# Second FFN of a decoder layer: products of a seven-product scheme ordered by kind, with shared sums in one PSUM bank

## The chip, the cores and the metric

The kernel runs on one core of one Trainium2 chip. The metric is device microseconds of one execution. Three runs of the kernel before took 2109.22, 2109.67 and 2110.75 us.

## The reference

One layer of a decoder over T = 272 positions (16 meta tokens and 256 tokens), width 2048, float32:

```
u = rms_norm(h, ffn1_norm_g);  h = h + 0.5 * swiglu(u, gate1, up1, down1)      # D_FF = 5632
u = rms_norm(h, mix_norm_g);   z = u @ w_in                                    # q k v, indexer, conv, gates
h = h + (sigmoid(ga) * y_attn + sigmoid(gc) * y_conv) @ w_out
u = rms_norm(h, ffn2_norm_g);  h = h + 0.5 * swiglu(u, gate2, up2, down2)
swiglu(x) = (silu(x @ w_gate) * (x @ w_up)) @ w_down
```

Only the last 256 positions are returned. The change is in the last line, the second FFN, which works on those 256 positions alone: two halves of 128 tokens.

## The kernel before, in words

**Products.** Every float32 operand is split into a high and a low part (`hi` a copy rounded to the matmul's type, `lo` what is left), and one product is three matmuls: hi·hi, hi·lo, lo·hi (`trio`, L407 to L410). In the second FFN the stationary operand is a 128x128 block of activations and the moving one 512 columns of weights.

**Quads.** The work is cut into quads: two 128-row blocks of the contraction, two token halves, two 512-column halves of the weights. A plain quad takes 8 products, 24 matmuls. A mixed quad uses the Winograd form of Strassen's scheme: 7 products P1 to P7, 21 matmuls, on sums of activations (`combos`, made in the kernel) and sums of weights (made by `job` during the earlier stages and kept in a scratch buffer in HBM, tiles `made` and `sums`).

**Stages.** The FFN's 5632 inner columns are taken in two groups (`GROUPS = 6, 5`). Each group has 6 or 5 up parts of 8 quads (gate columns and up columns together, 512 each), whose result is gated, transposed and kept in `mid`, and then two down parts (d = 0 and d = 2) of 12 or 10 quads that contract over `mid`. An up part's result f is used by quads 2f and 2f + 1 of the down parts. Before the change the first up part mixes quad 5, every other up part quads 1, 3, 5, 6, the down parts 4 and 4 (first group) and 3 and 5 (second): 57 mixed quads.

**The stream.** Weights come by SP's queue, 1 MB at a time at most, into four raw buffers (three `raw`, one `raws`; `load_one`, L152). A step of the stream (`subs`, `Stream.next`, L211) is up to two blocks of 128x512. `split` (L167 to L176) makes `whi` on ACT and then `wlo` on DVE, for the step three ahead of the one that PE is about to do; there are four pairs of split buffers. A plain step is 4 products (12 matmuls), a mixed step 2 products (6 matmuls), both of them 1024 columns to split. In the kernel before a mixed quad has four steps A to D, of which B is one block.

**Order on an engine.** Each engine runs its instructions in the order in which the program issues them. `st.put(fn, slot)` queues work by slots counted from the step at which it is called: slot 2k is issued at the begin of step k, before the split that step k issues (that of step k + 3), slot 2k + 1 behind that split. `LAG` holds the slots.

**Around the products.** `spread` (L764) adds the products P1, P5, P6, P7 of a part out of four PSUM banks of their own into the four quarters of `u`; `gather` (L776) adds those to the four result banks `c`: DVE, 1024 columns and twice 512. `silu` (ACT, twice 512), `times` (DVE, 1024 columns) and `turn_gated` with `move_blocks` (DVE transposes and DMAs by POOL) follow. The last up part of a group is transposed by DVE alone: `turn_columns` (L626; four transposes L513 in each of four calls, at `last_turn`), then `split_last` (L463 to L465, at `last_split`). `down_combos` makes the activation sums of the down parts: five DVE operations (L702 to L706) and, at a later slot, the split of the results (L689).

Of the kernel before, what the change touches and what calls it, by code (L numbers as in the profile page):

```python
# [67 lines left out]
MIXED = 1, 3, 5, 6  # L68
FIRST_MIXED = 5,
FIFTH = 4  # L70
FIVE = ()
LAST_MORE = 3, 4
JOBS_FROM = 24
JOBS_EVERY = 5
JOBS = 46
LATE_FROM = 4
LATE_EVERY = 6
DOWN_MIXED = {6: (6, 8, 9, 10), 5: (5, 6, 7)}
RAW = 2048
LAG = dict(  # L80
    spread=(0, 0, 1, 1), gather=(0, 0, 0), silu=(1, 1), times=(1,), turn=(1, 1), move=4, hi=(28, 33),
    lo=(28, 33), last_times=(1,), last_turn=(5, 5, 8, 10), last_split=12, half=(3, 3), drain=(2, 4, 3),
    act_combos=(4, 12, 19, 32), factors=(7, 10, 12), out=(1, 1, 5, 17), act_split=(9, 14, 25, 33),
    below=(12, 17, 22, 30, 34), below_split=(15, 20, 30, 34, 35), fifth=(22, 25), late_below=(0, 5),
    late_split=(0, 6),
# [3 lines left out]
def order(n, mixed):  # L89

    out, i = [], 0
    while i < n:
        if i not in mixed:
            out += [(i, "0"), (i, "1")]
        else:
            out += [(i, x) for x in "ABCD"]
        i += 1
    return out


def down_mixed(g, d):
    return sorted((*DOWN_MIXED[GROUPS[g]], *(LAST_MORE if g and d else ())))


class Stream:
# [28 lines left out]
    def add_part(self, name, src, made=None):  # L134

        def load(x):
            self.loads.append((x, x.shape[1], ()))
            return len(self.loads) - 1

        if name in "0A":  # L140
            self.own = load(src if name == "0" else src[:, HALF:]), name == "A" and load(made)
        g = self.own[name in "CD"]
        a, b = {"0": (0, 2), "1": (2, 4), "A": (0, 2), "B": (2, 3), "C": (0, 2), "D": (2, 4)}[name]
        self.subs.append((lambda: self.raw[g][:, a * HALF : b * HALF], b - a, HALF, (g,) if name in "1BD" else ()))
# [91 lines left out]
def tile_decoder_layer(  # L236
# [18 lines left out]
    wgu2: bass.AP,  # L255
    wd2: bass.AP,
# [30 lines left out]
    gu = down = 0  # L287
    made = []
    scratch = ctx.enter_context(tc.tile_pool(name="scratch", bufs=1, space=bass.MemoryType.DRAM))
    for g, n in enumerate(GROUPS):  # L290
        for f in range(n):
            now = sorted((*MIXED, *(FIFTH,) * ((g, f) in FIVE))) if gu else FIRST_MIXED
            sums = {i: scratch.tile([P, RAW], F32, name=f"made{gu + i}") for i in now}
            made += [(wgu2[gu + i], x) for i, x in sums.items()]
            for i, name in order(8, now):
                st.add_part(name, wgu2[gu + i], sums.get(i))
            gu += 8
        for d in (0, 2):
            now = down_mixed(g, d)
            sums = {i: scratch.tile([P, RAW], F32, name=f"sums{down + i}") for i in now}  # L300
            made += [(wd2[down + i], x) for i, x in sums.items()]
            for i, name in order(2 * n, now):
                st.add_part(name, wd2[down + i], sums.get(i))
            down += 2 * n
# [14 lines left out]
    rope = const.tile([P, 3, ROPE], F32, name="rope")  # L319
    cbias = const.tile([P, BOTH], F32, name="cbias")  # L320
    ident = const.tile([P, P], F32, name="ident")
    ones = const.tile([P, P], F32, name="ones")
    const.tile([P, 88], F32, name="fill")
# [19 lines left out]
    def tables():  # L343
# [5 lines left out]
    st.later(tables, 16)  # L349
# [57 lines left out]
    def trio(ps, x, w, first, last):  # L407
        nc.tensor.matmul(ps, x(0), w[0], start=first, stop=False)  # L408
        nc.tensor.matmul(ps, x(0), w[1], start=False, stop=False)  # L409
        nc.tensor.matmul(ps, x(1), w[0], start=False, stop=last)  # L410

    def quads(c, m, x, mixed, n, after_mixed, tail=False):

        def of(k, j):
            return lambda part: x(k, j, part)

        plan, joined = [], []
        for i, name in order(n, mixed):
            k = 2 * i
            if name in "01":  # L420
                unit = [(c[j, q], of(k + int(name), j), 1 - q) for j in (1, 2) for q in (1, 0)]
                if tail and i == n - 1:
                    unit = [] if name == "0" else [
                        (c[j, q], of(k + u, j), 2 * u + 1 - q) for j in (1, 2) for q in range(2) for u in range(2)
                    ]
            else:
                s1, s2, s3, s4 = (lambda part, q=q, i=i: mixed[i](q, part) for q in range(4))
                p1, p2, p3, p4 = (m[1], of(k, 1)), (c[1, 0], of(k + 1, 1)), (c[1, 1], s4), (c[2, 0], of(k + 1, 2))
                p5, p6, p7 = (m[5], s1), (m[6], s2), (m[7], s3)
                unit = dict(A=(p1, p3), B=(p2,), C=(p5, p6), D=(p7, p4))  # L430
                unit = [(*p, b) for b, p in enumerate(unit[name])]
            plan.append((unit, i == max(mixed) and name == "D"))
        flat = [id(p[0]) for unit, _ in plan for p in unit]
        at = 0
        blocks = []
        for unit, last in plan:
            blocks = blocks + [st.next()] + st.rest()
            for ps, xx, b in unit:
                trio(ps, xx, blocks[b], id(ps) not in flat[:at], id(ps) not in flat[at + 1 :])
                at += 1  # L440
            blocks = [] if unit else blocks
            if last:
                after_mixed()
# [110 lines left out]
    def job(pool, bufs, src, to, at, every, touch):  # L554
        box = {}

        def load():
            box["x"] = pool[0].tile([P, RAW], F32, name="made", bufs=bufs)
            if touch:
                nc.vector.tensor_copy(box["x"][:, :1], ones[:, :1])  # L560
            nc.gpsimd.dma_start(box["x"], src)

        def sums(n):
            b12, b11, b22, b21 = (box["x"][:, i * HALF : (i + 1) * HALF] for i in range(4))
# [8 lines left out]
        st.later(lambda: nc.gpsimd.dma_start(to, box["x"]), 1, at + every + 4)  # L573

    def ffn_features():
# [3 lines left out]
        with tc.tile_pool(name="ffn1", bufs=2, reuse_waits="tile") as fp:  # L579
# [16 lines left out]
            for i, (src, to) in enumerate(made[:JOBS]):  # L596
                job([fp], 3, src, to, st.at + JOBS_FROM + i * JOBS_EVERY - 1, JOBS_EVERY, i < 3)
# [56 lines left out]
    def ffn_tokens():  # L654

        with ExitStack() as pools:
# [4 lines left out]
            order_of = [*FIRST_MIXED, *(i for i in MIXED if i not in FIRST_MIXED)]  # L661
            comb = fp.tile([P, 3, 3, 2, P], F32R, name="comb")
            kept = {i: [comb[:, n, q] for q in range(3)] for n, i in enumerate(order_of[:3])}
            written = set()

            def known(key, x):
# [3 lines left out]
            mixed = {  # L670
                i: lambda q, part, i=i: known(i, kept[i][q - 1][:, part] if q else halves[:, 2 * i, part, 1])
                for i in MIXED
            }
# [18 lines left out]
            def put(fns, slots):  # L692
                for fn, slot in zip(fns, slots, strict=True):
                    st.put(fn, slot)
# [920 lines left out]
```

## Time and profile before

| | |
|---|---|
| median of three runs | 2109.67 us |
| span of the profiled execution | 2106.9 us |
| PE busy in it | 2098.8 us |
| DVE, ACT, POOL busy | 1582.4, 1058.9, 106.0 us |
| granted TensorE clock | 1.000 in the mean |
| HBM read, written | 504.90, 68.68 MB |

One execution was profiled, with a span of 2106.9 us from its first to its last instruction; the median run is 2.8 us longer, which is what lies around the span and the spread of the runs. Matmul durations overlap in this profile (one of 512 columns is shown as 0.39 us and the next one starts earlier), so the distance of their starts is what a matmul costs.

### The profile page before, as it was taken

How to read it: one execution, taken by the hardware profiler on the slowest of the kernel's cores; microseconds unless marked ns; L12 is line 12 of the kernel's file. 1: busy time of each engine (PE TensorE's matmuls, PEld its weight loads, DVE VectorE, ACT ScalarE, POOL GpSimd, SP SyncE). 2: the span in 40 equal slices, each digit the busy share in tenths (PEclk: the TensorE clock that was granted, in tenths of full speed). 3: DMA queues.
4: the chain of work that ended last, by engine and by line, in shares of the span. 5: the costliest groups of instructions: out<-in, count | busy, mean ns of one | idle time of the engine just before them, and what ended most of it. 6: DMA issues, size and time to landing. Idle time of an engine off the chain costs nothing.

```text
span 2106.9 us, 31863 instructions
## 1 busy us (share of the span) xinstructions
PE 2098.8 (100%) x12731; PEld 1889.9 (90%) x12731; DVE 1582.4 (75%) x2144; ACT 1058.9 (50%) x1342; POOL 106.0 (5%) x207
## 2 busy tenths in 40 slices
PE   9999999999999999999999999999999999999998
PEld 9999999999999999889988888888888888888887
DVE  7676766676776766578679678769788896878897
ACT  6444433344444445565444444456575565566654
POOL 0000000000000000000000000011000000000000
PEclk9999999999999999999999999999999999999999
DMA  7788888888888865445468886667988777799865
GB/s 265 260 320 327 324 315 322 311 337 310 322 313 325 328 224 177 164 159 181 152 216 329 323 301 223 219 233 255 314 314 300 281 268 247 282 306 319 306 250 207
DMA packets 85908, 575.64 MB, mean 273 GB/s; under 512 B 10112, under 2 KB 10880, under 8 KB 23808
## 3 DMA queue, kind: packets, MB, share of 16 engines
q1 hardware_dynamic: 64080, 438.34, 58.4%
q0 software_dynamic: 21104, 134.23, 17.1%
q8 instruction: 99, 1.62, 0.3%
q10 hardware_dynamic: 576, 1.05, 0.1%
q14 instruction: 49, 0.40, 0.1%
HBM read 504.90 MB, written 68.68 MB: 272 GB/s over the span
## 4 chain that ended last, share of the span: by engine, by line
PE 98%; DVE 1%; DMA 1%; issue 0%; ACT 0%; DVEq 0%; ACTq 0%
PE three L409 5%; PE three L408 5%; PE three L410 5%; PE pd L375 4%; PE pd L376 4%; PE pd L374 4%; PE pu L374 4%; PE pg L375 4%; PE pg L374 4%; PE pu L375 4%; PE pg L376 4%; PE pu L376 4%; PE pgt L402 3%; PE pgt L404 3%; PE pgt L403 3%; PE one L408 3%
## 5 line engine op out<-in xcount | busy, mean ns | idle before, releaser
L176 DVE TENSOR_TENSOR wlo<-raw,whi 128x1024 fp32r<-128x1024 f32 (+1 forms) x771 | 906.2, 1188 | 464.5 <-ACT whi L175 457.7
L175 ACT ACTIVATE whi<-raw 128x1024 fp32r<-128x1024 f32 (+1 forms) x771 | 786.4, 1030 | 883.4 <-PE pd L375 146.2
L375 PE MATMUL pd<-mid,whi 128*128 128x272 f32 x704 | 201.9, 287 | 0.0
L376 PE MATMUL pd<-mid,wlo 128*128 128x272 f32 x704 | 201.9, 287 | 0.0
L374 PE MATMUL pd<-mid,whi 128*128 128x272 f32 x704 | 201.9, 287 | 0.0
L374 PE MATMUL pu<-act,whi 128*128 128x272 f32 x672 | 192.8, 287 | 0.0
L376 PE MATMUL pu<-act,wlo 128*128 128x272 f32 x672 | 192.7, 287 | 0.0
L376 PE MATMUL pg<-act,wlo 128*128 128x272 f32 x672 | 192.7, 287 | 0.0
L375 PE MATMUL pg<-act,whi 128*128 128x272 f32 x672 | 192.7, 287 | 0.0
L375 PE MATMUL pu<-act,whi 128*128 128x272 f32 x672 | 192.7, 287 | 0.0
L374 PE MATMUL pg<-act,whi 128*128 128x272 f32 x672 | 192.7, 287 | 0.0
L568 DVE TENSOR_TENSOR made<-made 128x512 f32<-128x512 f32 x228 | 156.3, 685 | 0.0
L408 PE MATMUL three<-whi,act 128*128 128x512 f32 x352 | 137.2, 390 | 0.1
L409 PE MATMUL three<-wlo,act 128*128 128x512 f32 x352 | 137.0, 389 | 0.0
L410 PE MATMUL three<-whi,act 128*128 128x512 f32 x352 | 137.0, 389 | 0.0
L376 PEld LDWEIGHTS pd<-mid,wlo 128*128 128x128 f32 x704 | 132.7, 188 | 0.0
L374 PEld LDWEIGHTS pd<-mid,whi 128*128 128x128 f32 x704 | 132.7, 188 | 0.0
L375 PEld LDWEIGHTS pd<-mid,whi 128*128 128x128 f32 x704 | 132.7, 188 | 0.0
L176 DVE TENSOR_TENSOR wlo<-raws,whi 128x1024 fp32r<-128x1024 f32 x92 | 103.5, 1140 | 31.7 <-ACT whi L175 31.0
L374 PEld LDWEIGHTS pu<-act,whi 128*128 128x128 f32 x672 | 126.7, 188 | 0.0
L374 PEld LDWEIGHTS pg<-act,whi 128*128 128x128 f32 x672 | 126.7, 188 | 0.0
L376 PEld LDWEIGHTS pg<-act,wlo 128*128 128x128 f32 x672 | 126.6, 188 | 0.0
(381 smaller groups left out, 4482.7 us busy)
## 6 DMA issues: line engine op xcount, KB each, us to landing
raw<-in_wgu_dram SPq DMA_DIRECT2D x123, 1024.0 KB, 6.4
raw<-in_wd_dram SPq DMA_DIRECT2D x63, 1024.0 KB, 6.7
made<-in_wgu_dram POOLq DMA_DIRECT2D x41, 1024.0 KB, 10.6
made<-made POOLq DMA_DIRECT2D x41, 1024.0 KB, 6.5
raw<-made SPq DMA_DIRECT2D x31, 1024.0 KB, 6.1
raw<-in_wcv_dram SPq DMA_DIRECT2D x24, 1024.0 KB, 4.9
raw<-in_wgc_dram SPq DMA_DIRECT2D x24, 1024.0 KB, 5.1
raw<-in_wga_dram SPq DMA_DIRECT2D x24, 1024.0 KB, 5.4
```

The costliest lines, as they stand in the source:

```text
L175: nc.scalar.activation(hi[:, :n], raw, AF.Copy)
L176: nc.vector.tensor_sub(lo[:, :n], raw, hi[:, :n].bitcast(F32))
L374: nc.tensor.matmul(ps, whi, xhi, start=first, stop=False)
L375: nc.tensor.matmul(ps, whi, xlo, start=False, stop=False)
L376: nc.tensor.matmul(ps, wlo, xhi, start=False, stop=last)
L402: nc.tensor.matmul(ps, xhi, whi, start=k + i == 0, stop=False)
L403: nc.tensor.matmul(ps, xhi, wlo, start=False, stop=False)
L404: nc.tensor.matmul(ps, xlo, whi, start=False, stop=k + i == n - 1)
L408: nc.tensor.matmul(ps, x(0), w[0], start=first, stop=False)
L409: nc.tensor.matmul(ps, x(0), w[1], start=False, stop=False)
L410: nc.tensor.matmul(ps, x(1), w[0], start=False, stop=last)
L568: getattr(nc.vector, f"tensor_{op}")(to, a, b)
```

## The change

- `MIXED` is quads 0 to 3 of every up part but the first, which is plain; the down parts mix quads 0 to 3 each (`DOWN_MIXED`). That is 56 mixed quads.
- Within a part the mixed products come by kind: P1 of the four quads, P2 of the four, P6, P7, P5, P4, P3, two blocks in every step, and no step of one block. In an up part (`mixed_first`) they stand ahead of the plain quads, with P4 and P3 among the first of these; in a down part (`plain_first`) behind `lead` plain steps: 14 and 8 steps in the first group, 10 and 4 in the second.
- P1, P6, P5 (and P7 in the down parts) accumulate in one bank `m`; between kinds ACT copies it to a quarter of `u` (`copies`). In an up part `m` is the result bank `c[2, 1]`, and P7 starts in `c[2, 0]`. `spread`'s three DVE operations go; a down part gets two of 512 columns.
- Slots: `times` at 3, `turn_gated` and `move_blocks` in the plain steps of the next part, `last_turn` 9, 9, 11, 13 in place of 5, 5, 8, 10, `last_split` 14 in place of 12; the down sums of quad i at step 7 + 2i, their split at step 8 + 2i.
- Weights of the second FFN lie in HBM in the order of the stream (`w2`); the sums of a part lie in one scratch tile, by kind.

```
-MIXED = 1, 3, 5, 6
-FIRST_MIXED = 5,
-DOWN_MIXED = {6: (6, 8, 9, 10), 5: (5, 6, 7)}
+MIXED = 0, 1, 2, 3
+DOWN_MIXED = (4, 4), (4, 4)
-    spread=(0, 0, 1, 1), gather=(0, 0, 0), silu=(1, 1), times=(1,), turn=(1, 1), move=4, hi=(28, 33),
-    lo=(28, 33), last_times=(1,), last_turn=(5, 5, 8, 10), last_split=12, half=(3, 3), drain=(2, 4, 3),
-    below=(12, 17, 22, 30, 34), below_split=(15, 20, 30, 34, 35), fifth=(22, 25), late_below=(0, 5),
+    silu=(1, 1), times=(3,), last_turn=(9, 9, 11, 13), last_split=14, drain=(0, 2, 4), below=7,
...
+def mixed_first(mixed, plain):
+    own = in_twos(of_kind("P1", mixed) + of_kind("P2", mixed))
+    made = in_twos(sum((of_kind(x, mixed) for x in ("P6", "P7", "P5", "P4")), []))
+    rest = in_twos(of_kind("P3", mixed) + sum(plain_pairs(plain), []))
+    early = -(-3 * len(mixed) // 2)
+    seq = [("h", x) for x in own] + [("m", x) for x in made[:early]]
+    made = made[early:]
+    for i, x in enumerate(rest):
+        seq.append(("h", x))
+        if i >= 2 and i % 2 == 0 and made:
+            seq.append(("m", made.pop(0)))
+    return seq
+def plain_first(mixed, plain, lead):
+    pairs = plain_pairs(plain)
+    seq = [("h", x) for x in pairs[:lead]]
+    pairs = pairs[lead:]
+    seq += [("h", x) for x in in_twos(of_kind("P1", mixed) + of_kind("P2", mixed))]
+    for name in ("P6", "P7", "P5", "P4"):
+        seq += [("m", x) for x in in_twos(of_kind(name, mixed))]
+        if name in ("P6", "P7"):
+            seq.append(("h", pairs.pop(0)))
+    seq += [("h", x) for x in in_twos(of_kind("P3", mixed))]
+    return seq + [("h", x) for x in pairs]
...
+            out.append((("down", g, d), mixed, plain_first(mixed, plain, left - 2 if not d else left - 8)))
...
+            def copy(to, bank):
+                return lambda: st.put(lambda: nc.scalar.activation(u[:, to], bank, AF.Copy), 0)
...
+                        copies = dict(P1=copy(1, m), P6=copy(2, m), P7=copy(3, c[2, 0]), P5=copy(0, m))
...
+                for i in range(max(DOWN_MIXED[g])):
+                    at = LAG["below"] + 2 * i
+                    put_combos(middle, i, home(i), (g, i), 2 * at, 2 * at + 2)
...
+                    copies = dict(P1=copy(0, m), P6=copy(2, m), P7=copy(1, m), P5=after)
...
+        st.later(
+            lambda: nc.gpsimd.dma_start(to, box["x"].rearrange("p (t c) -> p t c", t=4)), 1, at + every + 4
+        )
```

## Rows read from the trace of the kernel before

**Rows 1.** The page, part 1: busy us (share of the span), instructions.
```profile
PE 2098.8 (100%) x12731; PEld 1889.9 (90%) x12731; DVE 1582.4 (75%) x2144; ACT 1058.9 (50%) x1342; POOL 106.0 (5%) x207
```
**Rows 2.** The page, part 4: the chain that ended last, by engine.
```profile
PE 98%; DVE 1%; DMA 1%; issue 0%; ACT 0%; DVEq 0%; ACTq 0%
```
**Rows 3.** Waits of PE: who for whom, us in total, times, longest.
```profile
PE three L409 <- DVE wlo L176: 1.1, 2, 0.8
PE three L408 <- ACT whi L175: 0.3, 1, 0.3
```
**Rows 4.** Timeline of PE, first and last of the second FFN: start, us, instruction.
```profile
1418.94 0.39 PE L408 MATMUL one<-whi,act 128*128 128x512 f32 x1
...
2101.14 0.39 PE L410 MATMUL two<-whi,mid 128*128 128x512 f32 x1
```
**Rows 5.** Chain in order of time: the same matmul of successive up parts.
```profile
1495.27 0.24 PE one L408
...
1576.94 0.24 PE one L408
```
**Rows 6.** Chain in order of time near 2072 us: a late load.
```profile
2072.36 8.25 DMA raw<-sums
```
**Rows 7.** Timeline of PE where one up part ends and the next begins.
```profile
1502.39 0.39 PE L410 MATMUL three<-whi,act 128*128 128x512 f32 x1
1502.62 0.39 PE L408 MATMUL one<-whi,act 128*128 128x512 f32 x1
```
**Rows 8.** Timeline of ACT there (idle before, and what ended it).
```profile
1502.82 0.64 ACT L175 ACTIVATE whi<-raw 128x512 fp32r<-128x512 f32 x1 [1.66 <-PE three L410]
1504.43 1.34 ACT L788 ACTIVATE few<-few,rcol 128x512 f32<-128x512 f32 x2 [0.98 <-DVE few L780]
1505.67 1.05 ACT L175 ACTIVATE whi<-raw 128x1024 fp32r<-128x1024 f32 x1
```
**Rows 9.** Timeline of DVE there: gather, and splits back to back.
```profile
1503.17 1.22 DVE L780 TENSOR_TENSOR few<-three,u 128x1024 f32<-128x1024 f32 x1
1504.31 0.68 DVE L781 TENSOR_TENSOR u<-one,u 128x512 f32<-128x512 f32 x1
1504.91 0.68 DVE L782 TENSOR_TENSOR u<-two,u 128x512 f32<-128x512 f32 x1
1505.50 0.68 DVE L176 TENSOR_TENSOR wlo<-raw,whi 128x512 fp32r<-128x512 f32 x1
...
1508.59 4.59 DVE L176 TENSOR_TENSOR wlo<-raw,whi 128x1024 fp32r<-128x1024 f32 x4
```
**Rows 10.** Timeline of ACT in the second group's first down part.
```profile
2001.40 1.06 ACT L175 ACTIVATE whi<-raw 128x1024 fp32r<-128x1024 f32 x1 [1.41 <-PE three L410]
...
2013.40 1.06 ACT L464 ACTIVATE mid<-mt 128x1024 fp32r<-128x1024 f32 x1 [2.83 <-DVE mt L513]
```
**Rows 11.** Timeline of DVE there: transposes, last split, sums of quad 5.
```profile
2002.50 1.22 DVE L176 TENSOR_TENSOR wlo<-raw,whi 128x1024 fp32r<-128x1024 f32 x1 [0.23 <-ACT whi L175]
2003.64 3.57 DVE L513 STREAM_TRANSPOSE mt<-few 32x256 f32<-32x256 f32 x8
...
2014.54 1.22 DVE L465 TENSOR_TENSOR mid<-mt,mid 128x1024 fp32r<-128x1024 f32 x1
2015.67 0.69 DVE L702 TENSOR_TENSOR few<-mid 128x512 f32<-128x512 f32 x1
...
2017.33 1.22 DVE L176 TENSOR_TENSOR wlo<-raws,whi 128x1024 fp32r<-128x1024 f32 x1
...
2019.60 0.29 DVE L689 TENSOR_TENSOR mid<-few,mid 128x128 fp32r<-128x128 f32 x1
...
2020.27 0.69 DVE L176 TENSOR_TENSOR wlo<-raw,whi 128x512 fp32r<-128x512 f32 x1
```
**Rows 12.** Busy time by stretch: us, engines, PEclk, DMA share, GB/s.
```profile
1484.30:1489.80 5.50, 5.50 (x26) 4.57 (x25) 2.84 (x4) 3.26 (x4) 0.00 (x0) 1.00 1.01 425
2064.00:2080.00 16.00, 16.00 (x72) 13.26 (x71) 12.52 (x12) 10.06 (x11) 0.00 (x0) 1.00 0.82 260
```
**Rows 13.** Waits of POOL: its stores of weight sums.
```profile
POOL made L573 <- DVE made L568: 541.5, 41, 14.3
```

More of the change, by code (lines that the diff above doesn't have):

```diff
@@ L89, in order @@
[L89 to L97, printed above, removed]
-    return out
-def down_mixed(g, d):
-    return sorted((*DOWN_MIXED[GROUPS[g]], *(LAST_MORE if g and d else ())))
+    silu=(1, 1), times=(3,), last_turn=(9, 9, 11, 13), last_split=14, drain=(0, 2, 4), below=7,
+    act_combos=(6, 10, 14, 18, 23), act_split=(9, 13, 17, 21, 25), factors=(7, 10, 12), out=(1, 1, 5, 17),
+)
@@ L105, with loads_of @@
+def loads_of(seq):
+    loads, open_of = [], {}
+    for at, (kind, blocks) in enumerate(seq):
+        x = open_of.get(kind)
+        full = x and sum(len(seq[i][1]) for i in x[1]) + len(blocks) > RAW // HALF
+        if x is None or full or at - x[1][-1] > 4:
+            x = open_of[kind] = (kind, [])
+            loads.append(x)
+        x[1].append(at)
+    return loads
 class Stream:
@@ L132, in add, with add_plan @@
             self.subs.append((view, b - a, width, (g,) if b == n else ()))
[L134 to L144, printed above, removed]
+    def add_plan(self, seq, host, made):
+        at = 0
+        where = {}
+        for kind, subs in loads_of(seq):
+            n = sum(len(seq[i][1]) for i in subs) * HALF
+            if kind == "h":
+                src = host(n)
+            else:
+                src, at = made[:, at : at + n], at + n
+            g = len(self.loads)
+            self.loads.append((src, n, ()))
+            a = 0
+            for i in subs:
+                where[i] = g, a, (g,) if i == subs[-1] else ()
+                a += len(seq[i][1])
+        for i, (_, blocks) in enumerate(seq):
+            g, a, done = where[i]
+            n = len(blocks)
+            self.subs.append((lambda g=g, a=a, n=n: self.raw[g][:, a * HALF : (a + n) * HALF], n, HALF, done))
     def load_one(self, between=(), queues=()):
@@ L405, in tokens, with trio @@
             k += len(blocks)
[L407 to L412, printed above, removed]
+    def trio(ps, x, w, first, last, halting):
+        for i, (a, b) in enumerate(((0, 0), (0, 1), (1, 0))):
+            nc.tensor.matmul(
+                ps, x(a), w[b], start=first and i == 0, stop=last and i == 2, skip_group_check=halting
+            )
@@ L414, in of, with quads @@
+    def quads(c, m, x, s, mixed, seq, copies, last=False):
         def of(k, j):
             return lambda part: x(k, j, part)
[L417 to L425, printed above, removed]
-            else:
[L427 to L432, printed above, removed]
@@ L738, in down_combos @@
[L738 to L746 removed]
+                )
+                his, los, _ = home()
@@ new lines, in combos, with of_combos, of, view @@
+                return sums, split
+            def of_combos(x, home, key):
+                def of(i, q):
+                    def view(part):
+                        if not q:
+                            return known(key(i), x[:, 2 * i, part, 1])
+                        return known(key(i), home(i)()[2](q, part))
+                    return view
+                return of
+            def put_combos(x, i, home, key, slot, late):
+                sums, split = combos(x, i, home, key)
+                for fn in sums:
+                    st.put(fn, slot)
+                st.put(split, late)
```

413 lines of the change are left out of this document (234 added, 179 removed).

## The prediction

> **What bounds the kernel now.** I read the page's busy times first: PE is busy for all but 8 of 2106.9 us, DVE for three quarters [rows 1]. The chain of waits says the same: 98% of what ends last is PE [rows 2]. Then the waits of PE: in the whole second FFN it stood idle for 1.4 us [rows 3]. So a change here can gain little, unless it takes matmuls away, and can lose as much as it makes PE wait. Next comes the price of a matmul, from starts. The same matmul of two up parts lies 1576.94 - 1495.27 = 81.67 us apart over two parts [rows 5]. A part with 4 mixed and 4 plain quads has 4 x 21 + 4 x 24 = 180 matmuls, so one costs 81.67 / 360 = 0.227 us. A mixed step (6 matmuls) is 1.36 us, a plain one (12) 2.72 us. The 57 mixed quads of 132 make 132 x 24 - 57 x 3 = 2997 matmuls. Their starts span 2101.14 - 1418.94 = 682.2 us [rows 4]; 2996 x 0.2269 = 679.7, so 2.5 us are waits. The largest lies behind one late load [rows 6].
>
> **What the change does to PE's own work.** One mixed quad fewer is 3 matmuls more: 3 x 0.227 = +0.7 us. Nothing else changes PE's work. Taking away all 2.5 us of old waits gives -2.5: the places where they stood are laid out anew, and what waits there next is counted below. The other end is that they all stay (0).
>
> **Where steps can be late.** PE needs a step's `wlo` at the step's second matmul. The chain behind that: a split buffer comes free when PE ends a step, and ACT starts on it 1502.82 - 1502.62 = 0.20 us after the next step's first matmul [rows 7, 8]. `whi` takes 1.06 [rows 10], and DVE takes 4.59 / 4 = 1.15 us a piece back to back [rows 9]. With four buffers there are three steps of time. Mixed steps leave DVE only 1.36 - 1.15 = 0.2 us each, plain ones 1.57. So what DVE has to do besides counts where mixed steps stand, and the change puts them together: up to twelve in a row at the start of an up part (four P1 and P2, six of P6, P7, P5, two P3), six in a row in a down part.
>
> **Term 1, from mixed up part to up part (8 times: 4 in each group).** Zero is the first matmul of the new part. DVE may start `gather` at 0.20: 1.14, then twice 0.60 (starts 1503.17, 1504.31, 1504.91, 1505.50 [rows 9]): 2.54. The split of step 3, 1.14: 3.68. ACT meanwhile: `whi` of step 3; `silu` when the first sum is there, 0.20 + 1.22 + 0.04 = 1.46; the two take 1505.67 - 1504.43 = 1.24 [rows 8]: 2.70; `whi` of step 4 until 3.76. DVE: `wlo` 4 from 3.79 to 4.93; then `times`, which the change issues behind it (slot 3): 1.14, 6.07; `wlo` 5 is done at 6.07 + 1.22 = 7.29, handed on at 7.35. PE wants it at 5 x 1.36 + 0.23 = 7.04: **0.3 us late, 8 times: 2.4 us**. In the kernel before two plain steps lay here. Step 6 is in time (DVE gains 0.2 a step). The bounds: 0, if DVE keeps 0.05 us less on each of these six, and 0.6, if it loses as much. The copies of `m` (ACT, as `silu` 0.6) are covered: between a kind's end and the next write of the bank stand two mixed or one plain step, 2.7 us. The three DVE additions that go stood in plain steps, so they give nothing back.
>
> **Term 2, first down part of the second group, the last up part's result.** Its quad 8 is plain and needs up part 4, the last one. It stands at steps 8 and 9 of the ten plain steps ahead. The transposes are issued behind the split of step 7 (slot 9: step 4) and later. Zero is the part's first matmul. Step 3 ends at 4 x 2.72 = 10.90; `whi` of step 7 starts at 11.10. From there on I lay the old trace over it: `whi` 2001.40, `wlo` 2002.50, transposes 2003.64, `split_last` on ACT 2013.40 to 2014.46, on DVE 2014.54 to 2015.76 [rows 10, 11]. The same two splits stand between the sixteen transposes after the change (slots 9, 9, 11, 13). So the transposes start at 11.10 + 2.24 = 13.34, the high half is there at 13.34 + (2014.46 - 2003.64) = 24.16, the low half at 25.46. PE comes to step 8 at 21.8. It waits until 24.2, runs two matmuls, and waits at the third for the low half from 24.66 to 25.5: 2.4 + 0.85 = **3.3 us**. Before, the transposes stood two steps earlier and nothing wanted their result so soon. Bounds 2.4 (the first wait alone) and 3.7.
>
> **Term 3, the same part, the activation sums.** Behind `split_last` DVE has, from 25.4 on, four times the five sums (2017.33 - 2015.67 = 1.66), four times their split (2020.27 - 2019.60 = 0.67) [rows 11], and the `wlo` of steps 10 to 16 between them (7 x 1.14): 6.64 + 2.68 + 7.98 = 17.3, so the sums of quad 3 are split at 42.7. PE ends step 8 at 24.2 + 0.85 + 2.72 = 27.8, step 9 at 30.5, the five mixed steps 10 to 14 at 37.3, and wants quad 3's sum for P6 in the middle of step 15, at 38.0. **4.8 us** of waits between steps 10 and 15. Bounds: 3.5, were the operations 7% shorter; 6.5, as DVE may also have to wait for ACT in that string (the copy of P1 stands behind a split that waits for DVE).
>
> **Term 4, first down part of the first group.** The same string, but with 14 plain steps ahead, and the last up part is first wanted at step 12 (32.7): no wait as in term 2. `wlo` 10 is there at 25.4 + 1.66 + 1.22 = 28.3, wanted at 27.5: 0.8. `wlo` 16 is there at 42.1, wanted, with that shift, at 41.9: 0.2; `wlo` 17, behind quad 3's split in four pieces, at 44.1, wanted at 43.5: 0.6. **1.6 us**, bounds 0.5 and 2.5.
>
> **At nothing.** The first part has DVE's sums in sixteen plain steps. The stores of the weight sums fall into four pieces a row; POOL waits 541.5 us for DVE ahead of those stores [rows 13], and they are wanted hundreds of us later. If that cover were gone, a job would be late, not PE. The end of the kernel is ordered as before.
>
> **Sum.** +0.7 - 2.5 + 2.4 + 3.3 + 4.8 + 1.6 = +10.3 us. Against the profiled execution's 2106.9 that is 2117.2; runs take 2109.67 - 2106.9 = 2.8 more: **2120 us**, +0.5%.
>
> **Loads, and a page against the row.** A mixed step eats 128 x 1024 x 4 bytes in 1.36 us, 385 GB/s, twelve times in a row (6.3 MB), with up to four raw buffers of 1 MB loaded ahead. The trace has 425 GB/s over 5.5 us, but also 260 over 16 us [rows 12], the stretch with the late load. The Trainium skill ("DMA: Bandwidth & Descriptors", Specifications) gives a core some 358 GB/s of HBM; by it the twelve steps would take 17.6 us for 16.3, 1.2 us late in each of 9 up parts, some 11 us, if nothing lay ahead. The 425 speak against that limit here, with one core at work.
>
> **Rivals.**
> - *The string starts earlier* (not slower). If DVE gets to the sixteen transposes two plain steps sooner than I place them (5.4 us), as in the kernel before with slots 5, 5, 8, 10, term 2 and 4 vanish and term 3 too (4.8 < 5.4): +0.7 - 2.5 + 2.4 = +0.6, 2110.3 us. From some 2.5 us on the result is within 0.2% (2.4 + 0.8 + 2.3 - 1.8 = +3.7). For it: the old layout had next to no wait [rows 3]. Against: the diff's slots 9, 9, 11, 13 and the order of DVE.
> - *Loads become the bound.* A wait of 1.4 us, as much as PE idles now in all [rows 3], in each of the 13 mixed parts is +18: with the walked terms 2138, with half of them 2133. For it: 385 wanted, 260 seen. Against: that stretch had five mixed quads with loads of 0.75 and 1 MB; now all are of 1 MB, and plain steps need half as much.
> - *Half of the walk*: terms 1 and 4 are covered, 2 and 3 stay: 2109.7 - 1.8 + 8.1 = 2116.
> - *The mix doesn't bind at all*: no new wait, 2109.7 - 1.8 = 2107.9. That is the floor, and it is within 0.2%: to be faster by that, matmuls would have to start closer than 0.227 us.
>
> **Chances.** About 0.2% (4.2 us) is what a measurement of this kernel tells from no change. As walked 0.60, half of it 0.10, loads 0.10: slower 0.80. Earlier string 0.12, nothing binds 0.04: same 0.16. For a gain that I don't see, faster 0.04. The bounds of the terms give +0.7 - 2.5 + 0 + 2.4 + 3.5 + 0.5 = +4.6 (2114.3) to +0.7 + 4.8 + 3.7 + 6.5 + 2.5 = +18.2 (2127.9). The range for 8 in 10 reaches a little to both other cases: 2112 to 2130.
>
> **What would show it.** Starts of 0.227 us and 3000 matmuls; in each mixed up part but the first a wait of PE for `wlo` at step 5 of some 0.3 us; in the second group's first down part, 22 us behind its begin, a wait for the result of `split_last`, and 8 to 14 us later one for `wlo` or the sums, together 8 us. Wrong, if PE's waits there are under 3 us, if PE waits for raw loads, or if the gain or loss lies ahead of 1419 us.

## The result, and the profile after

The changed kernel takes 2125.12 us (median of 4 runs, 2124.39 to 2126.23), the kernel before 2110.21 on the same chip (4 runs): the ratio is 1.0075, with a 95% interval of 1.0061 to 1.0089. Slower, as forecast, at 2125 where 2120 was said. The traced execution is the one of 2126.23 us.

The page of the changed kernel, its busy times, answers [rows 1], and its chain [rows 2]:

```profile
PE 2108.2 (99%) x12734; PEld 1891.4 (89%) x12734; DVE 1544.3 (73%) x2062; ACT 1072.1 (50%) x1349; POOL 116.1 (5%) x205
```

Its chain that ended last, by engine:

```profile
PE 93%; DVE 4%; issue 2%; ACT 1%; DMA 0%; DVEq 0%; ACTq 0%
```

DVE has 38 us less to do than before and yet a larger part of the chain, 4% for 1%. It isn't how much it has to do, but when. PE's waits in the changed kernel (us in total, times, longest), which answer [rows 3]:

```profile
PE single L470 <- ACT mid L541: 2.3, 1, 2.3
PE single L470 <- DVE wlo L238: 2.1, 5, 0.7
PE single L470 <- ACT act L794: 1.5, 1, 1.5
...
PE single L470 <- DVE mid L542: 0.5, 1, 0.5
PE single L470 <- DVE act L796: 0.5, 1, 0.5
PE double L470 <- DVE wlo L238: 0.3, 1, 0.3
```

L470 is the matmul of the second FFN, L238 the low half of a weight split, L541 and L542 the two halves of `split_last`, L794 and L796 those of the activation sums. No row is a wait for a load. These rows make 7.2 us, and the loss is 15. The rest is seen only in the distance of the starts. First and last matmul of the second FFN (timeline of PE in the changed kernel), which answer [rows 4]:

```profile
1419.47 0.39 PE L470 MATMUL single<-whi,act 128*128 128x512 f32 x1
...
2118.33 0.39 PE L470 MATMUL single<-whi,mid 128*128 128x512 f32 x1
```

3000 starts span 698.9 us for 682.2 before. At 0.2269 us each, what single starts lie further apart than that (where it is more than 0.02 us) sums to 17.9 us, for 2.6 before; taken from the whole span, 698.9 - 2999 x 0.2269, it is 18.4. By place, from the timeline of PE:

| place | us |
|---|---|
| eight transitions from mixed to mixed up part, 0.41 each | 3.3 |
| first mixed up part, steps 4 and 5 | 1.5 |
| first group, first down part | 1.7 |
| second group, first down part: waits for `split_last` | 3.3 |
| the same part: waits in P6 | 3.2 |
| the same part: two stretches in which TensorE ran at half its clock | 4.5 |
| second group, second down part | 0.5 |

**The second group's first down part.** PE in the changed kernel's timeline, the first matmul of the part and then the wait:

```profile
2003.60 0.39 PE L470 MATMUL single<-whi,mid 128*128 128x512 f32 x1
...
2025.13 0.39 PE L470 MATMUL double<-whi,mid 128*128 128x512 f32 x1
2027.78 0.50 PE L470 MATMUL single<-whi,mid 128*128 128x512 f32 x1 [2.26 <-ACT mid L541]
2028.12 0.40 PE L470 MATMUL single<-wlo,mid 128*128 128x512 f32 x1
2029.04 0.79 PE L470 MATMUL single<-whi,mid 128*128 128x512 f32 x1 [0.52 <-DVE mid L542]
2029.63 0.63 PE L470 MATMUL double<-whi,mid 128*128 128x512 f32 x1
2030.06 0.63 PE L470 MATMUL double<-wlo,mid 128*128 128x512 f32 x1
```

DVE there, its transposes, a split between them and the low half of `split_last`, which answer [rows 11]:

```profile
2016.91 3.57 DVE L590 STREAM_TRANSPOSE mt<-few 32x256 f32<-32x256 f32 x8
2020.51 1.22 DVE L238 TENSOR_TENSOR wlo<-raw,whi 128x1024 fp32r<-128x1024 f32 x1
...
2027.76 1.22 DVE L542 TENSOR_TENSOR mid<-mt,mid 128x1024 fp32r<-128x1024 f32 x1 [1.12 <-ACT mid L541]
```

The transposes begin 13.31 us into the part (2016.91 - 2003.60; walked 13.34), PE goes on 24.18 us in (walked 24.2) and gets the low half 25.44 us in (walked 25.46). From the row at 2029.04 on starts lie 0.43 us apart: 2029.63, 2030.06. That is no wait. The windows of the changed kernel say what it is (busy us by engine, PEclk, DMA share, GB/s):

```profile
2024.00:2028.00 4.00, 1.74 (x8) 1.16 (x7) 2.81 (x6) 1.33 (x2) 0.00 (x0) 1.00 0.53 166
2028.00:2032.00 4.00, 3.48 (x9) 2.46 (x9) 3.93 (x9) 2.31 (x4) 0.00 (x0) 0.55 0.23 96
2044.00:2048.00 4.00, 1.73 (x6) 0.60 (x4) 3.93 (x10) 2.31 (x5) 0.00 (x0) 1.00 0.61 199
2048.00:2052.00 4.00, 3.94 (x11) 3.17 (x12) 3.41 (x4) 2.13 (x3) 0.00 (x0) 0.61 0.15 64
```

Behind each stretch in which PE stood for more than half of the time (busy 1.74 and 1.73 of 4 us), the granted clock is down to 0.55 and 0.61 of full in the mean over the next 4 us: in part of them it is at half, 1.2 of 2.4 GHz. Some 14 matmuls behind the first wait and 8 behind the second cost 0.2 us more each, 2.9 + 1.6 = 4.5 us. Before, the clock was 1.00 throughout the second FFN.

**A transition.** The third up part of the first group begins at 1505.41. DVE there, in the timeline of the changed kernel, which answers [rows 9]:

```profile
1505.61 1.23 DVE L875 TENSOR_TENSOR few<-double,u 128x1024 f32<-128x1024 f32 x1 [0.40 <-PE double L470]
...
1510.34 1.22 DVE L892 TENSOR_TENSOR few<-u,few 128x1024 f32<-128x1024 f32 x1
1511.47 1.22 DVE L238 TENSOR_TENSOR wlo<-raws,whi 128x1024 fp32r<-128x1024 f32 x1
```

PE six microseconds on, at step 5 of the part:

```profile
1511.98 0.61 PE L470 MATMUL single<-whi,comb 128*128 128x512 f32 x2
1512.74 0.50 PE L470 MATMUL single<-wlo,comb 128*128 128x512 f32 x1
1513.09 0.40 PE L470 MATMUL single<-whi,comb 128*128 128x512 f32 x1
```

`times` (L892) starts 4.93 us into the part, as walked to the hundredth, and the split of step 5 follows it. PE has two starts by 1512.21 and wants the next at 1512.44; it comes at 1512.74, 0.30 us late. But the one behind it comes only 0.35 us later, not 0.227. That second loss, 0.11 to 0.12 us, stands behind every wait here. The view of waits lists none of the eight: PE is shown busy for 0.61 us from 1511.98, so only 0.15 us of idle time is left in it.

**The first mixed up part**, ACT in the changed kernel's timeline:

```profile
1463.19 1.06 ACT L237 ACTIVATE whi<-raws 128x1024 fp32r<-128x1024 f32 x1 [1.66 <-PE double L470]
1464.27 1.28 ACT L884 ACT_TABLE_LOAD   x1
1465.57 1.27 ACT L884 ACTIVATE few<-double,rcol 128x512 f32<-128x512 f32 x2
```

The first Silu needs a table load of 1.28 us. In the timeline of ACT in the kernel before it stands at the same place, ahead of plain steps, and cost nothing:

```profile
1462.69 1.28 ACT L788 ACT_TABLE_LOAD   x1
```

Now mixed steps follow, and PE waits 0.53 and 0.95 us for their `wlo`. The Trainium skill ("ScalarE: Activation LUTs", What ACT_TABLE_LOAD costs) puts a switch at some 2.66 us, 1.28 for the load and 1.38 for a drain. The row agrees on the load and shows no drain: the split ahead of it ends, and the Silu behind it begins, within 0.02 us of it.

### The profile page after: what moved, and what is told of

Read it like the earlier page. It is cut to its first block, busy times and chain, and to the rows that moved or that the text cites. A ratio compares the mean times of both kernels' runs of the same rounds, so it can differ in the third digit from the quotient of the medians.

```text
span 2124.5 us, 31659 instructions
## 1 busy us (share of the span) xinstructions
PE 2108.2 (99%) x12734; PEld 1891.4 (89%) x12734; DVE 1544.3 (73%) x2062; ACT 1072.1 (50%) x1349; POOL 116.1 (5%) x205
## 4 chain that ended last, share of the span: by engine, by line
PE 93%; DVE 4%; issue 2%; ACT 1%; DMA 0%; DVEq 0%; ACTq 0%
PE single L470 14%; PE double L470 12%; PE pd L437 4%; PE pd L435 4%; PE pd L436 4%; PE pg L436 4%; PE pu L436 4%; PE pu L437 4%; PE pg L437 4%; PE pg L435 4%; PE pu L435 4%; PE pgt L463 3%; PE pgt L465 3%; PE pgt L464 3%; DVE wlo L238 2%
## 5 line engine op out<-in xcount | busy, mean ns | idle before, releaser
L238 DVE TENSOR_TENSOR wlo<-raw,whi 128x1024 fp32r<-128x1024 f32 (+1 forms) x747 | 903.9, 1218 | 507.8 <-ACT whi L237 503.2
L470 PE MATMUL single<-whi,act 128*128 128x512 f32 x592 | 218.0, 389 | 2.0 <-ACT act L794 1.5
L470 PE MATMUL double<-whi,act 128*128 128x512 f32 x544 | 200.3, 389 | 0.0
L470 PEld LDWEIGHTS single<-whi,act 128*128 128x128 f32 x592 | 111.1, 188 | 26.1 <-ACT act L794 1.9
L238 DVE TENSOR_TENSOR wlo<-raws,whi 128x1024 fp32r<-128x1024 f32 x86 | 104.5, 1221 | 32.1 <-ACT whi L237 31.1
L436 PEld LDWEIGHTS pu<-act,whi 128*128 128x128 f32 x672 | 126.6, 188 | 0.0
L435 PEld LDWEIGHTS pu<-act,whi 128*128 128x128 f32 x672 | 126.6, 188 | 0.0
```

What stands on the lines that cost most here:

```text
L238: nc.vector.tensor_sub(lo[:, :n], raw, hi[:, :n].bitcast(F32))
L435: nc.tensor.matmul(ps, whi, xhi, start=first, stop=False)
L436: nc.tensor.matmul(ps, whi, xlo, start=False, stop=False)
L470: nc.tensor.matmul(ps, x(a), w[b], start=first and i == 0, stop=last and i == 2, skip_group_check=halting)
```

## The experiments

The theory: the loss is PE's waits for work of DVE and ACT that now stands too late, each of which another order can cover, and the lower clock is a consequence of the longest of them. The rival: DVE's string of work as a whole sets the pace, and to mend one wait only moves it. Another: the half clock belongs to the mixed steps themselves. On the chip of the first four experiments the kernel before took 2108.2 us, so the changed one, which wasn't run there, would take an estimated 2108.2 x 1.0075 = 2124.0. The waits and the excess are those of one traced execution each. "Excess" is the sum that was 17.9 us above.

**`times` later in mixed up parts.**
```
-  put(times(None if mixed else c), LAG["times"])
+  put(times(None if mixed else c), (11,) if mixed else LAG["times"])
```


> The changed kernel (2125.1 us) with one slot moved: the multiplication `times` of a mixed up part at slot 11 (behind the split issued at step 5) in place of 3. Theory: at the begin of a mixed up part DVE is what is late (gather 2.3 us and times 1.1 us beside splits of 1.14 in steps of 1.36); with times four steps later the 0.41 us waits of PE at step 5 go in all eight parts: -3.3 us, 2121.8, and the trace shows PE waits under 0.1 us there. Rival, the loads are late there: the waits stay, 2125.

2120.77 us, ratio 1.0059 (1.0044 to 1.0074); excess 13.2. All eight waits are gone, 3.3 us. So term 1 is what it was taken for: `times` ahead of the split of step 5. The first of the two stretches at half clock, 2.9 us, is gone too, though the edit doesn't touch it and the wait of 3.3 us in front of it is still there. Of these 2.9 us, 1.4 come back further on in PE's timeline, because PE now reaches P6 earlier:

```profile
2037.03 0.50 PE L470 MATMUL single<-whi,act 128*128 128x512 f32 x1 [1.15 <-ACT u L866]
```

L866 is ACT's copy of the shared bank, and in ACT's order it stands behind the split of an activation sum that waits for DVE.

**The table of Silu loaded early**, by a Silu of two numbers where the norm's factors are made.
```
+  nc.scalar.activation(sums[:, 3], rcol[:, 0, :2], AF.Silu)
```


> The changed kernel with one tiny Silu on two columns added on ACT in the plain steps of the first up part, so that the table load of 1.28 us does not stand before the first real Silu. Theory: the 1.48 us that PE waits at the begin of the first mixed up part (the one stall there that was not foreseen) come from that table load on ACT, which delays whi: they fall to some 0.1 us, -1.4 us, 2123.7. Rival, they come from putting the mixed steps together and DVE's share: they stay, 2125.

2122.25 us, ratio 1.0066 (1.0049 to 1.0083); excess 15.3. The 1.48 us are 0.10 (0.17 more stand in the first part); the transitions stay at 0.42; here too there is one stretch at half clock, not two. The table load was the cause. Two of the four executions of this kernel have a mean clock of 1.000 and no room for such a stretch (the traced one has 0.999): whether the clock falls differs from one execution to the next, so some 1.5 us of any one excess can be chance.

**The last transposes and split one step earlier.**
```
-  last_turn=(9, 9, 11, 13), last_split=14
+  last_turn=(7, 7, 9, 11), last_split=12
```


> The changed kernel with the last up part's transposes and split one plain step (2.72 us) earlier: last_turn 7, 7, 9, 11 and last_split 12. Theory: in the second group's first down part the result of split_last is then there at 21.5 us for the high half (wanted 21.8) and 22.8 for the low (wanted 22.3): the wait of 3.4 us falls to some 0.5, and the TensorE clock, which fell to its lower level behind it for 6.8 us and cost some 2.9 us, does not fall there; behind it the waits for the sums grow, since PE comes earlier, from 3.1 to about 5 us, still with a fall of the clock (1.5 us). In the first group's first down part 1.7 us of waits become under 0.5. Sum -5 us, 2120. Rival, the string of DVE as a whole sets the time and an earlier begin only moves the wait: the two places together (11.0 us now) stay within 1.5 us of that, 2124. Rival, the fall of the clock has nothing to do with the wait: it falls at the same place all the same.

2121.70 us, ratio 1.0063 (1.0048 to 1.0078); excess 13.5. The first group's 1.66 are 0.18, and the second group's wait for `split_last` is 0.67 for 3.33. But behind it 0.57 and 0.43 are new, and P6 has 1.54 and 4.75 (with one stretch at half clock) where the two kernels above have 1.45 and 4.75: of the 2.7 us that an earlier begin gave back at `split_last`, 1.1 are lost again. The two places together make 8.0 us, for 11.0 in the changed kernel and 9.5 in the two runs above, which have one stretch at half clock as well. By the rival they stay within 1.5 us of 11.0: that is refuted by 8.0, but half of the 3.0 us is the stretch at half clock that those two runs lack as well. In time it is 2.3 us under 2124.0, for 4 expected; the four executions lie between 2119.60 (clock 1.000) and 2122.82 (0.998).

**The second group's sums of quads 2 and 3 left out** (their products take those of quads 0 and 1, so part of the result is not the reference's).
```
+  if g and i > 1:
+      continue
...
```


> The changed kernel with half of the activation sums of the second group's down parts left out (quads 2 and 3 use the sums of quads 0 and 1, so part of the computation is wrong). Theory: the waits at P6 (3.1 us, and 1.5 us of the lower clock behind them) come from DVE's sums of quads 2 and 3: they go, -4.5 us, 2120.6; the wait for split_last ahead of it and the lower clock behind that (6.2 us) stay. Rival, they come from the splits of the six mixed steps in a row: most of the 4.7 us stays, 2124.

2119.79 us, ratio 1.0056 (1.0041 to 1.0071); excess 11.9. No wait is left in P6; `split_last` keeps its 3.3 us, now with a stretch at half clock of 1.6 us behind it. Term 3 is DVE's sums: with two of the four left out, ACT's copy of the shared bank comes in time as well.

**All covers at once.** The first three edits in one (`last_turn` 7, 9, 11, 13, `last_split` 15; the second group's sums a step later), and another order for the second group's first down part, in which P4 and P3, which don't use the shared bank, stand between the kinds that do:
```
+  seq = [("h", x) for x in pairs[:8]]
+  seq += [("h", x) for x in in_twos(of_kind("P1", mixed) + of_kind("P2", mixed))]
+  seq += [("h", x) for x in pairs[8:]]
+  for name in ("P6", "P4", "P7", "P3", "P5"):
+      seq += [("h" if name == "P3" else "m", x) for x in in_twos(of_kind(name, mixed))]
```
In this run and the next two, that part's weight sums were still stored in the old order of kinds, so P4, P7 and P5 took one another's; a later run puts that right.

> All covers at once on the changed kernel: the times of the mixed up parts at slot 11, the table of Silu loaded early, last turns at 7, 9, 11, 13 and last split at 15, and in the second group's first down part eight plain steps, P1, P2, the four other plain steps, then P6, P4, P7, P3, P5, so that P6 starts 8 plain steps + 4 mixed + 4 plain = 38 us into the part instead of 33, and each shared bank has another kind between its uses; its sums of the activations start one step later. Theory (the loss is waits of the tensor engine for work of VectorE that stands too late, each coverable, and the lower clock is a consequence of them): waits in the second FFN fall from 14 us to about 2.5, no stretch at the lower clock is left, and the time goes to within 0.2% of the kernel before (0.9985 to 1.002), some 15 us under the changed kernel. Rival (VectorE's string as a whole sets it, and a wait only moves): 4 us or more of waits stay, ratio 1.003 or more. Rival (the lower clock comes from the mixed stretches themselves): a stretch at half clock stays although no wait of over 1 us is left.

2110.42 us, ratio 1.0009 (1.0000 to 1.0018); excess 2.6, as before the change. PE's waits in the second FFN of this kernel:

```profile
PE single L481 <- ACT u L877: 0.7, 1, 0.7
PE double L481 <- DVE wlo L249: 0.7, 1, 0.7
```

Its chain that ended last, by engine:

```profile
PE 98%; DVE 1%; issue 0%; ACT 0%; DVEq 0%; POOL 0%; POOLq 0%
```

The clock is 1.00 throughout the second FFN, with as many mixed steps in a row in the up parts as in the changed kernel, and with ten in a row in the down part where it fell before. So nearly every wait could be covered, and the mixed steps alone don't lower the clock. The first of the two rows is ACT's copy of the shared bank ahead of the next part, 1.0 us by the starts.

**That order alone.** Only the five lines above (and the drains that follow from them).

> The changed kernel with the second group's first down part alone in the other order (eight plain steps, P1, P2, four plain steps, P6, P4, P7, P3, P5). Theory: the waits before P6, P7 and P5 (4.7 us beside the lower clock) lose the part that the later start of P6 (+5.4 us) and the kinds between them cover, to about 2; the wait for the last split, 3.3 us at step 8, stays, since the eight plain steps ahead of it are the same ones; the eight transitions (3.3) and the table load (1.4) stay. So 2.5 to 5 us under the changed kernel, ratio 1.005 to 1.0065 against the kernel before, most of the spread from whether the clock falls once or not. Rival (VectorE's string as a whole sets it): the later waits grow to what the earlier ones lose, ratio 1.0075.

2120.55 us, ratio 1.0062 (1.0047 to 1.0077); excess 13.9. The size is as said, the way to it isn't. I said that the wait for `split_last` stays; but the quads that need it now come after P1 and P2, so it is gone, and P2's `wlo` is late instead, in the waits of this kernel:

```profile
PE double L481 <- DVE wlo L249: 2.9, 2, 2.6
```

With half clock behind it that place costs 6.5 us; P6, P7 and P5 have no wait, and 0.96 stands where the next part reuses the bank. DVE's string is still late; it now meets PE elsewhere.

**Five of eight quads mixed**, with all covers.
```
-  MIXED = 0, 1, 2, 3
+  MIXED = 0, 1, 2, 3, 4
...
-EARLY = 0
+EARLY = 3
...
-    rest = in_twos(of_kind("P3", mixed) + sum(plain_pairs(plain), []))
+    rest = in_twos(of_kind("P3", mixed)) + plain_pairs(plain)
```
`EARLY` puts three of the ten more jobs for weight sums into an earlier stage; the last line keeps the fifth P3 in a step of its own.

> The kernel with all covers and five of eight quads mixed in the ten mixed up parts instead of four: 10 x 3 = 30 fewer matmuls of 0.227 us, -6.8 us; 10 x 3 more blocks to load (0.26 MB each) and to split, and ten more jobs that store weight sums earlier in the kernel. Theory (the covers hold and the loads, 425 GB/s in steps in a row, keep up with 47 blocks in 40 us, 306 GB/s): 6 to 7 us under the kernel with all covers, ratio 0.995 to 0.999. Rival (loads or the splits of VectorE become late in 17 mixed steps in a row): waits of the tensor engine for raw loads or wlo in each of the ten parts, 0.5 us each or more, and a ratio of 1.0 or above. Rival (the later jobs disturb the stages before): the second FFN begins later than in the kernel with all covers by over 1 us.

2121.63 us (2116.96 to 2122.66), ratio 1.0061 (1.0046 to 1.0076): 11 us over the kernel with all covers, though it runs 30 matmuls fewer. Its second FFN takes 690.3 us (1423.03 to 2113.32) for 683.5, with waits of 0.2 us or more in each up part but the first group's first two and 3.9 us at one place of the second group's first down part, with a stretch at half clock. It begins 3.5 us later, the sign of the second rival, that the later jobs disturb the stages before. In the second FFN PE waits for `wlo`, DVE for ACT, and ACT for loads. Who ACT waited for up to 2010 us (us, times, longest), with five quads mixed:

```profile
ACT whi L248 <- DMA raw<-sums_up: 17.9, 15, 2.2
...
ACT whi L248 <- DMA raw<-in_w_dram: 8.1, 7, 2.4
```

The same with four:

```profile
ACT whi L248 <- DMA raw<-in_w_dram: 4.7, 5, 1.5
...
ACT whi L248 <- DMA raw<-sums_up: 1.7, 4, 0.7
```

Over 1503 to 1543 us the DMA engines are busy for 0.90 of the time at 323 GB/s, with four quads for 0.88 at 310. ACT waits 26.0 us for these two kinds of load with five quads, 6.4 with four. The chain ahead of one of PE's waits (1571.27, 0.76 us in the view) runs through such a load, in order of time:

```profile
1559.38 2.28 DVE wlo L249 x2
...
1561.67 7.12 DMA raw<-sums_up
...
1568.90 1.07 ACT whi L248
```

The load is issued when DVE is through with a raw buffer, and ACT starts when it has landed. That points to the loads, which the prediction held for harmless: they are so with four mixed quads, and hardly with five. A kernel that eases the loads alone wasn't run, so their share of the loss is not shown, nor is what the later jobs cost.

**The kernel before with a later last split**, to see the clock behind a wait amid other products, in two runs.
```
-  last_split=12
+  last_split=14
```


> The kernel BEFORE with the last split of each group one step later (slot 14 instead of 12), nothing else: one wait of the tensor engine of 2.5 to 3.3 us in each group's first down part, in place of 0.8 in the second, beside plain products all around. Theory (a wait of about 3 us can be followed by a stretch at half clock, whatever products stand around it): +4 to +6 us for the waits, and a fall of the granted clock behind one of them or both adds 1.5 us each, ratio 1.002 to 1.0045. Rival (the lower clock belongs to the mixed steps): the same waits, clock 1.00 behind both.

2108.41 us, ratio 1.0000 (0.9991 to 1.0010).
```
-  last_split=12
+  last_split=30
```


> The kernel BEFORE with the last split of each group put nine steps later (slot 30), the last place ahead of its first use in the first group: the tensor engine has to wait there for a copy of 1.0 us on ACT, a subtraction of 1.15 us on DVE and what stands ahead of them, 2.5 to 4 us in the first group's first down part; in the second group's, the same or nothing. Theory (a fall of the granted clock follows a wait of some 3 us, whatever products stand around it): a stretch at half clock of 3.41 or 6.83 us behind such a wait, +1.5 or +2.9 us; ratio 1.0015 to 1.006. Rival (it belongs to the mixed steps in a row, two loads and splits per 1.36 us): the wait, and clock 1.00 behind it.

2109.16 us, ratio 1.0002 (0.9993 to 1.0012). PE's waits in the second FFN of this kernel:

```profile
PE three L409 <- DVE wlo L176: 1.8, 3, 0.8
```

Neither made the long wait that I expected (4 to 6 us of waits in the first, 2.5 to 4 in the second): the order before had nine steps to spare there, so these two tell nothing of the clock. They tell how much room the change took away.

**All covers, with the weight sums read in the order of the kinds.** The place of a load in the store is taken from its kind:
```
-  src, at = made[:, at : at + n], at + n
+  name, i = seq[subs[0]][1][0]
+  a = (("P6", "P7", "P5", "P4").index(name) * width + i) * HALF
+  src = made[:, a : a + n]
```


> The kernel with all covers, with the made blocks read in the order of the kinds as they now come (P6, P4, P7, P5): the same instructions, only the places of four loads in the store of the weight sums differ. Theory: as the kernel with all covers before, ratio 0.999 to 1.002, waits of the tensor engine in the second FFN 2.6 us, no stretch at the lower clock within it. Rival (the four loads' order mattered): a wait for a raw load, ratio over 1.002.

2110.55 us, ratio 1.0009 (0.9999 to 1.0018); excess 2.7. This is the change without its loss, and no gain on the kernel before.

**All covers but that order.**

> All covers but the order of the kinds: times at slot 11, the table early, last turns at 7, 9, 11, 13, last split at 15, sums of the second group one step later, and the changed kernel's own order of the second group's first down part. Theory: the eight transitions, the table load and the first group's down part lose their waits (-3.3, -1.4, -1.5); in the second group's first down part the split_last wait (3.3) and the waits before P6 (1.5 and 3.2) stay in sum at 6 to 8 us, as the early turns alone left them, with one or two falls of the clock of 1.5 us each: 2115 to 2118, ratio 1.0035 to 1.005. The difference to the kernel with all covers, 5 to 8 us, is then the order's worth. Rival (the early covers alone do it): ratio under 1.002.

2117.49 us, ratio 1.0041 (1.0026 to 1.0056); excess 9.7, of which 2.0 at `split_last` and 7.0 in P6 with half clock, within what was said. That is 7 us over the mended kernel until the order changes too: the order needs the covers, and the covers the order.

**One wait put back into the mended kernel.**
```
-  last_split=15
+  last_split=23
```


> The kernel with all covers, with one wait put back by itself: the last split of each group at slot 23 instead of 15, half a step ahead of the step that reads it, so that the tensor engine stands for 4 to 5 us at the thirteenth step of the second group's first down part (0.5 us in the first group's), and nothing else is late. Theory (the clock falls behind a long wait of the tensor engine): a stretch at half clock of 3.41 or 6.83 us begins within some microseconds behind that wait, 1.5 or 2.9 us dearer in starts of matmuls; 2.6 + 3 to 4 of waits, ratio 1.0025 to 1.004 with the fall. Rival (a wait alone doesn't do it; the changed kernel's falls need several waits near each other): the wait, the granted clock at 1.00 behind it, ratio 1.002 to 1.003.

2118.78 us, ratio 1.0053 (1.0036 to 1.0070); excess 10.6. Dearer than said: the first group's wait came out at 1.97 us, not 0.5, with the clock at 1.00 behind it. PE in this kernel's timeline, at the second group's wait:

```profile
2026.08 0.39 PE L483 MATMUL double<-whi,mid 128*128 128x512 f32 x1
2030.76 0.79 PE L483 MATMUL single<-whi,mid 128*128 128x512 f32 x1 [4.29 <-ACT mid L554]
2031.35 0.63 PE L483 MATMUL single<-wlo,mid 128*128 128x512 f32 x1
2032.39 0.80 PE L483 MATMUL single<-whi,mid 128*128 128x512 f32 x1 [0.41 <-DVE mid L555]
...
2033.41 0.63 PE L483 MATMUL double<-wlo,mid 128*128 128x512 f32 x1
2033.84 0.63 PE L483 MATMUL double<-whi,mid 128*128 128x512 f32 x1
```

The windows around it (columns as above):

```profile
2024.00:2028.00 4.00, 2.47 (x11) 1.69 (x10) 3.93 (x9) 2.91 (x5) 0.00 (x0) 1.00 0.54 172
2028.00:2032.00 4.00, 1.22 (x2) 0.50 (x2) 4.00 (x7) 3.36 (x4) 0.00 (x0) 0.64 0.62 207
2032.00:2036.00 4.00, 3.61 (x9) 2.85 (x10) 3.73 (x9) 0.83 (x2) 0.00 (x0) 0.50 0.35 145
```

One wait of 4.3 us (with 0.4 for the low half behind it), plain steps after it, and the clock falls to half; in the mended kernel, without it, it doesn't. All four executions have a mean clock of 0.998, those of the mended kernel 1.000, one of ten 0.999. That the wait is the cause here is shown. The fall comes while PE still stands: a mean of 0.64 over 2028 to 2032 is 2.9 us at half, and PE starts again only 1.2 us before the end of that stretch, with the next start 0.59 us later.

## Why the prediction was right, and where it fell short

- **The sign and the reason were right.** PE does the forecast matmuls at 0.227 us, where the clock is full, and loses what it waits for DVE, in part through ACT; the order of that work decides, for DVE has 38 us less of it. That all covers bring the time back to 1.0009 shows it.
- **Three more matmuls, old waits gone** (+0.7, -2.5): 3000 in the trace; none of the old waits is left.
- **Term 1** (2.4): 3.3. The lateness was 0.30 us each, as walked; what was missing is the 0.11 us that TensorE loses on the start behind a wait.
- **Term 2** (3.3): 3.3, and each of its times within 0.03 us.
- **Term 3** (4.8): 3.2 in the changed kernel, where the slower clock in front of it left DVE more time, and 1.4 + 3.2 = 4.6 in the run with `times` moved, which has no half clock ahead of it. The 1.43 are a wait for ACT's copy of P1, the path that the prediction has in its upper bound, and not for DVE directly. The run without half of the sums shows that they are the cause. The second wait of the sign came 18 us behind the first, not 8 to 14, and the two make 6.5 us, not 8.
- **Term 4** (1.6): 0.92 + 0.18 + 0.56 = 1.7.
- **The copies of the shared bank**, held for covered: so in the changed kernel, but not once PE came earlier (1.43 us above), nor ahead of the next part in the mended one (1.0 us).
- **At nothing: the end of the kernel, the weight sums' stores** as said (the end takes 0.4 us longer); **the first part** not. The walk began the first mixed up part's ACT work with `silu` as in every other one, and there the first Silu brings its table load: 1.5 us. The row was in the trace of before, at 1462.69.
- **Not foreseen: the clock**, 4.5 us. In the trace of before it was 1.00 in the second FFN, and no wait there exceeded 0.8 us; the walk priced each wait at its own length. Of the 4.5 us, 1.4 took the place of a wait in P6, as the run with `times` moved shows.
- **Rivals.** That the string of DVE starts earlier, that nothing binds, and half of the walk are refuted by the table of places. Loads as the bound: no wait of PE with four mixed quads, though with five they are the likeliest. Over twelve mixed steps in a row (1505.40 to 1521.70 in the changed kernel) the DMA moved 280 GB/s for the 385 that they use; the rest had been loaded ahead. The counts there are a little off, without bearing on the sum: there are 10 mixed up parts and 4 mixed down parts, not 9 and 13, the 2133 comes to 2132, and "each mixed up part but the first" makes nine places where term 1 has eight.
- **The sum.** The profiled span is 2124.5 for 2117.2 said, +7.3: clock 4.5, table 1.5, term 1 0.9, second down part 0.5, term 3 -1.6, and 1.5 that belongs to none (the second FFN begins 0.5 us later and the kernel's end behind it takes 0.4 longer; the rest is within the rounding of 0.227). The median of the runs lies 0.6 us over the span, not 2.8, which takes 2.2 off again: 2125.1 for 2120.0. That is chance: each run takes 1.7 or 1.8 us more than its own span, and here the traced execution was the slowest of the four.
- **Luck.** The four terms measure 11.5 us for 12.1 walked. What moved the result by 5 us are things that the sum hasn't, the clock and the table; that 2125 still lies in the range is owed to the width of the terms' bounds, none of which was meant for them.

What stays open: which waits bring the clock down. The traced stretch has two falls in the changed kernel and one in the runs with `times` or the table moved, behind the same waits, and executions of one kernel differ in it.

## What to carry to other kernels

Where TensorE has no slack, a reordering is priced by walking the helper engine's queue against PE's start times, place by place; such a walk hit the begin of the late work here to 0.03 us in two places, and what it missed were things that are not in the steady pattern: a first call's table load, the restart behind a wait, the clock behind a long one. Shared accumulators cost little (1.0 us here) if kinds that don't use them stand between those that do, and if the inputs of the dearest kind come early; mending one wait alone can just show the next. Before more of a cheaper scheme is used, see what its loads leave: with 0.88 of the DMA time taken in one up part, one more quad of the cheaper kind made the kernel slower, for which the loads are the likeliest cause.

## What the runs showed of the hardware

- The granted clock of TensorE falls to half (1.2 of 2.4 GHz) in or behind waits of 1.5 to 4.3 us, and 512-column matmuls then start 0.43 us apart for 0.227: once or twice in the second FFN of the changed kernel and of eight variants, never in the traces of the kernel before or the mended one, where no single wait in the view exceeds 0.8 us. Not each such wait does it. The run with `times` moved had 3.3 us of waits at 2021 and kept its clock, in these windows:

```profile
2020.00:2024.00 4.00, 1.74 (x9) 1.13 (x8) 2.81 (x6) 1.24 (x2) 0.00 (x0) 1.00 0.53 158
2024.00:2028.00 4.00, 3.47 (x14) 2.53 (x15) 3.93 (x9) 2.31 (x4) 0.00 (x0) 1.00 0.25 104
```

- Behind a wait at full clock, TensorE's second start comes 0.33 to 0.35 us after the first, for 0.227: each such wait costs 0.11 us more than its length.
- In this profile a wait of 0.3 us can be missing from the view of waits, eight times over: only the distance of the starts shows it.
